# Attention on one core: an order table in place of a planner, a tenth group of exponentials on VectorE, reciprocals as steps of their own, and the last head in two PSUM tiles

## The chip, the cores and the metric

The kernel runs on one core of a Trainium2 chip. The metric is the device time of one execution in microseconds (us), the median of several runs. A profiled execution gives the trace that is read here; its span goes from the first to the last instruction in the trace, and its own time is a little longer than the span.

A core has five engines that run beside each other, each with its own queue in a fixed order. TensorE (PE in the profile; PEld is its weight load) multiplies matrices into PSUM. ScalarE (ACT) computes the exponential. VectorE (DVE) and GpSimd (POOL) do elementwise work; GpSimd works in SBUF here. SyncE (SP) issues the DMA transfers. Engines wait for each other by semaphores.

## The reference

```
batch, heads, seq, dim = 8, 8, 512, 64        # q, k, v in float32
scale = 1.0 / np.sqrt(q.shape[-1])
scores = np.einsum('bhqd,bhkd->bhqk', q, k) * scale
scores = scores - scores.max(axis=-1, keepdims=True)
attn = np.exp(scores)
attn = attn / attn.sum(axis=-1, keepdims=True)
return np.einsum('bhqk,bhkd->bhqd', attn, v).astype(np.float32)
```

There are 64 independent heads. For each, a 512x512 table of scores is made, its exponential taken, and the rows are weighted with v and divided by their sums. The kernel does not subtract the maximum: the division takes out any common factor.

## The kernel before

Heads go in 32 pairs (g = 0 to 31). For a pair, q, k and v are loaded as fp32 (256 KB each, seven buffers each), and POOL casts them to fp16 (`cast`): k and q into one tile `qkp` (five buffers), v into one of twelve tiles `vps`, which have a column of ones beside the 64 columns of v. PE transposes k and q into PSUM (`transposes`, in two parts of four matmuls, part 0 for k, part 1 for q), and VectorE copies both to SBUF as `tqk` (`copy`). Pair 0 has a start of its own (`first_pair`). For pair 1 the two parts have two PSUM tiles and two copies, and the cast of its q is shared: half on VectorE, half on POOL.

Scores are made in *groups* of two 128x512 blocks (`scores`): keys on the partitions, queries along the row, four chunks c of keys per head. There are four groups per pair, 128 in all; the last one is done in two halves of the queries, so that they are numbered 0 to 128. A group's scores lie in one PSUM tile `st`, of which there are three; a fourth group must wait until the first has been read.

For most groups ScalarE takes the exponential from PSUM to a tile `pt` in SBUF (line 516). For a few groups, listed in `ON_DVE`, VectorE does it instead: PE adds a constant by one more matmul (`lift`, line 497), VectorE brings the scores into fixed range (`raise_`, `R`, tile z, line 536) and then makes four *passes* over them (`pass_`, line 553, tiles y and pd), all with fp32 data; a pass reads SBUF and writes SBUF.

The output is made in *units* of 128 queries of a head (`values`): four matmuls add up the chunks, and the column of ones gives the sum of the exponentials. Seven units share a PSUM tile `o`, of which there are two, in banks that the transposes use too. When a tile is full, `normalise` takes the reciprocals of the seven sums and multiplies (lines 566 and 568) into a ring of 56 units in SBUF, and every head that is then complete is stored by a DMA on SP's queue (line 577). The last head (pair 31, second head) has a PSUM tile of its own, taken from the score tiles (`last_values`, line 603): parts 0 and 1 add chunk 0 and 1 for all queries, parts 2 and 3 chunks 2 and 3 for each half of the queries, and `finish` (lines 617 and 618) normalises and stores each half, the first on SP's queue, the second on ScalarE's.

The order in which all of this is issued on each engine is written by a planner in the kernel (`Plan`), which steps through an assumed time, keeps assumed costs and due times, and emits one step after the other. The order on each engine is the order of the emitted steps that use it. `cast_behind` adds to most casts a wait for the VectorE instruction emitted last (`latest`), so that a cast begins at a chosen place between VectorE's instructions. `emit` gives after each cast the load that will use the same buffer, seven pairs later, and `plan.first_loads` is the order of the loads at the start.

Of the kernel before, what the change touches and what calls it, by code (L numbers as in the profile page):

```python
# [17 lines left out]
class Plan:  # L18

    SLOT, EXP, EXP_DONE, EXP_FIXED = 216, 853, 181, 50  # L20
    INTO, OUT_OF = 95, 105
    TRANSPOSE, V_UNIT = 225, 130
    TO_ACT, TO_DVE, TO_PE = 220, 210, 60

    COPY, NORM, RAISE = (601, 690), (307, 390), (1132, 1215)
    COPY_1 = (400, 190)
    NORM_COLUMN, PASS_DONE = 67, 80
    PASS, PASSES = 1133, 4
    OFFSET = 216
    FIRST_EXP = 4915  # L30
    STEP = 5
    CALM, KEEN = 9000, 4
    FIRST_UNIT = 4
    ON_DVE = (8, 24, 35, 41, 61, 68, 80, 94, 111)

    LATE_NORM, LATE_COPY, HURRY, SOON, BACKLOG = 1300, 1400, 900, 80, 1000
    SLACK, AHEAD = 0, 1

    CAST, CAST_DONE, TO_POOL = 557, 130, 150
    FIRST_LAND, LOAD, STORE, LATENCY, ISSUE = 5200, 700, 350, 2300, 450  # L40
    RAW, QK16, NV = 7, 5, 12

    def __init__(self, groups, pairs, first):
        self.groups, self.pairs = groups, pairs
        self.pe, self.act, self.dve = 7000, self.FIRST_EXP, 6300
        self.pool, self.port, self.dma = 4600, 4600, self.FIRST_LAND
        self.m, self.tiled = first, True
        self.read = []
        self.exps = {}
        for m in range(first):  # L50
            self.act += self.EXP + self.EXP_FIXED
            self.exps[m] = self.act + self.EXP_DONE
            self.read.append(self.exps[m])
        self.tq = {0: 5800}
        self.transposed = {0: 5800}
        self.next_t = 1
        self.part_t = 0
        self.banks = [5100, 5800]
        self.todo = [(g, h) for g in range(pairs) for h in range(2)]
        self.last = self.todo.pop()  # L60
        self.last_part = 0
        self.head = None
        self.units = self.FIRST_UNIT
        self.member = {b: m for m, grp in enumerate(groups) for b in grp}
        self.ready = []
        self.passes = []
        self.steps = []
        self.busy_dve = 0
        self.done_heads = 0

        late = {grp[0][0] for m, grp in enumerate(groups) if m in self.ON_DVE}
        due = []
        for g in range(pairs):
            scores = 5000 + 3380 * g
            if g:
                due += [(scores - 2300, g, "k"), (scores - 2290, g, "q")]
            due.append((scores + 4000 + (6000 if g in late else 0), g, "v"))
        self.due = sorted(due)
        self.uncast = list(self.due)
        self.casts = []  # L80
        self.landed, self.cast_done = {}, {}
        self.first_loads = [(g, n) for _, g, n in self.due if g < self.RAW]
        self.first_loads += [(self.RAW, "k"), (self.RAW, "q")]
        for x in self.first_loads:
            self.dma += self.LOAD
            self.landed[x] = self.dma
        self.loads = []
        self.sp = 1650 + 470 * len(self.first_loads)

    def note(self, t, *what):  # L90
        self.steps.append((t, len(self.steps)) + what)

    def emit(self, t, after):
        _, g, n = self.uncast.pop(0)
        shared = (g, n) == (1, "q")
        self.note(t, "cast", g, n, t > self.CALM)
        if not shared:
            self.casts.append((g, n, t if after is None else after + self.TO_POOL))
        if g + self.RAW < self.pairs:
            self.note(t, "load", g + self.RAW, n)  # L100
            self.loads.append(("load", g + self.RAW, n))

    def fits(self, t, soon=0):
        if not self.uncast:
            return False
        _, g, n = self.uncast[0]
        if n != "v" and g >= self.QK16 and self.transposed.get(g - self.QK16, 1e9) > t:
            return False
        return self.landed.get((g, n), 1e9) <= t + soon

    def step_pool(self, t):
        if self.uncast and self.uncast[0][1:] != (1, "q") and not self.casts and self.pool <= t:
            quiet = not self.passes and self.port <= t and not any(x[1] == "raise" for x in self.ready)
            if self.fits(t) and (quiet or self.uncast[0][0] - 1500 < t):
                self.emit(t, None)
        if self.casts and self.pool <= t and self.port <= t:
            g, n, after = self.casts[0]
            if after <= t and self.landed.get((g, n), 1e9) <= t:
                self.casts.pop(0)
                self.pool = t + self.CAST  # L120
                self.port = t + self.CAST
                self.cast_done[(g, n)] = t + self.CAST + self.CAST_DONE

    def step_sp(self, t):
        if not self.loads or self.sp > t:
            return
        what = self.loads[0]
        if what[0] == "load":
            _, g, n = what
            if g >= self.RAW and self.cast_done.get((g - self.RAW, n), 1e9) > t:  # L130
                return
            self.dma = max(self.dma, t + self.LATENCY - self.LOAD) + self.LOAD
            self.landed[(g, n)] = self.dma
        else:
            if what[1] > t:
                return
            self.dma = max(self.dma, t + self.LATENCY - self.STORE) + self.STORE
        self.loads.pop(0)
        self.sp = t + self.ISSUE

    def free(self, n=0):
        m = self.m + n
        if m >= len(self.groups):
            return 1e9
        g = self.groups[m][0][0]
        return max(0 if m < 3 else self.read[m - 3], self.tq.get(g, 1e9))

    def for_dve(self, m):
        return m in self.ON_DVE

    def scores(self, t):
        m, grp = self.m, self.groups[self.m]
        half = m >= len(self.groups) - 2
        slots = 2 if 0 < grp[0][0] and grp[0][2] == grp[1][2] and not half else 1
        on_dve = self.for_dve(m)
        self.note(t, "scores", m, on_dve)
        t += (0 if self.tiled else self.INTO) + self.SLOT * slots
        self.tiled = True
        if on_dve:
            t += self.OFFSET  # L160
            self.ready.append((t + self.TO_DVE, "raise", (m,)))
            self.read.append(1e9)
        else:
            begin = max(self.act, t + self.TO_ACT)
            self.idle = getattr(self, "idle", 0) + begin - self.act
            self.act = begin + self.EXP // (2 if half else 1) + self.EXP_FIXED
            self.exps[m] = self.act + self.EXP_DONE
            self.read.append(self.exps[m])
        self.m += 1
        self.pe = t  # L170

    def full(self, t, cost):
        self.pe = t + cost + (self.OUT_OF if self.tiled else 0)
        self.tiled = False

    def bank(self, t):
        n = min(range(2), key=lambda n: self.banks[n])
        return n if self.banks[n] <= t + 40 else None

    def transposes(self, t):  # L180
        if self.part_t == 0:
            self.bank_t = self.bank(t)
            self.banks[self.bank_t] = 1e9
        self.note(t, "transposes", self.next_t, self.part_t, self.bank_t)
        self.full(t, self.TRANSPOSE)
        self.part_t += 1
        if self.part_t == 2:
            self.transposed[self.next_t] = self.pe + self.TO_DVE
            self.ready.append((self.pe + self.TO_DVE, "copy", (self.next_t, self.bank_t)))
            self.next_t += 1  # L190
            self.part_t = 0

    def wants(self, g, h, part):
        members = [self.member[(g, c, h)] for c in range(4)]
        if (g, h) == self.last:
            end = len(self.groups)
            members = [(members[0], members[1], end - 2, end - 1)[part]]
        exps = max(self.exps.get(m, 1e9) for m in members)
        return max(exps, self.cast_done.get((g, "v"), 1e9))

    def edge(self):

        u, first = self.units, self.FIRST_UNIT
# [15 lines left out]
    def values(self, t):  # L219
        if self.last_values(t):  # L220
            return True
# [563 lines left out]
```

## Time and profile before

| | |
|---|---|
| median of 3 runs | 120.78 us (120.76 to 121.13) |
| profiled execution, its own time | 120.37 us |
| its span | 118.6 us |
| TensorE clock granted, mean | 0.993 |
| DMA | 33.83 MB, mean 285 GB/s |
| exponentials on ScalarE, line 516 | x117, 106.7 us busy |
| passes and raises on VectorE, lines 553 and 536 | x45, 56.4 us busy |
| copies of transposed pairs, line 482 | x30, 20.5 us busy |
| multiplications, line 568, and reciprocals, line 566 | x37 each, 22.6 and 7.3 us busy |
| casts on POOL, lines 435 and 445 | x93, 57.3 us busy |

How to read it: the page gives for each engine its busy time as a share of the span, then groups of instructions by line with their count, total and mean length. A line of the timeline has the start in us, the length in us, the engine, the line of the code, the operation, what it writes and what it reads, and how many instructions are merged; in brackets stands how long the engine was idle just before, and what ended that. An instruction's length is longer than what it costs its engine where the next one starts before it has ended; the distance from start to start is the cost.

### The profile page before, as it was taken

The numbers are of one execution on the slowest core, as the hardware profiler recorded it, in microseconds if no ns is written. First come the engines' busy times: TensorE is split into PE (matmuls) and PEld (weight loads), VectorE is DVE, ScalarE is ACT, GpSimd is POOL, SyncE is SP. The second block draws the span as 40 slices with busy tenths as digits, with TensorE's granted clock in tenths as the row PEclk, the third lists the DMA queues.
The fourth block names the chain that finished last, engine by engine and source line by source line (L and its number), as shares of the span: only waits on it lengthen the run. The fifth ranks groups of instructions, "written<-read, shape, count | busy, mean of one in ns | idle before, by whom it ended". The sixth has DMA issues, their size and how long they took to land.

```text
span 118.6 us, 4088 instructions
## 1 busy us (share of the span) xinstructions
PE 105.0 (89%) x1577; PEld 66.4 (56%) x1577; DVE 103.7 (87%) x179; ACT 111.6 (94%) x124; POOL 57.5 (48%) x102
## 2 busy tenths in 40 slices
PE   7969987999799897989989998998899998998960
PEld 2626554755466454658545574675465674755750
DVE  3453999799999999998999999999999999998560
ACT  4699999999999999999999999999999999999960
POOL 2378731991547722555947255533645436524000
PEclk9999999999999999999999999999999999999997
DMA  3999999999999999999889957999899874231344
GB/s 101 305 352 380 378 380 383 383 379 378 367 302 326 350 365 355 327 371 358 250 297 275 299 169 255 342 364 293 266 309 373 275 253 164 91 122 63 109 163 134
DMA packets 35607, 33.83 MB, mean 285 GB/s; under 512 B 2691, under 2 KB 35587, under 8 KB 35587
## 3 DMA queue, kind: packets, MB, share of 16 engines
q1 hardware_dynamic: 35152, 33.24, 84.8%
q10 hardware_dynamic: 432, 0.33, 0.8%
q8 instruction: 12, 0.20, 0.8%
q14 instruction: 11, 0.07, 0.2%
HBM read 25.17 MB, written 8.39 MB: 283 GB/s over the span
## 4 chain that ended last, share of the span: by engine, by line
ACT 34%; PE 28%; DVE 16%; DMA 11%; issue 6%; SPq 1%; POOL 1%; ACTq 0%
ACT pt L516 32%; PE o L588 10%; PE st L511 10%; DMA k<-in_k_dram 8%; DVE y L553 5%; PE tp L469 4%; DVE tqk L482 3%; DVE ring L568 3%; DMA out_dram<-ring 3%; PE st_0a L636 3%; ACT pt L686 2%; DVE z L536 1%; DVE rc L566 1%; DVE pd L553 1%; SPq L429 1%
## 5 line engine op out<-in xcount | busy, mean ns | idle before, releaser
L516 ACT ACTIVATE pt<-st 128x1024 f16<-128x1024 f32 (+1 forms) x117 | 106.7, 1200 | 0.1
L511 PE MATMUL st<-tqk 64*128 64x512 f16 (+1 forms) x250 | 45.3, 379 | 7.1 <-ACT pt L516 5.4
L588 PE MATMUL o<-vp,pt 128*128 128x65 f16 x936 | 41.7, 194 | 0.0
L588 PEld LDWEIGHTS <-pt 128*128 128x128 f16 x936 | 35.4, 98 | 11.2 <-issue 8.5
L445 POOL CAST qkp<-k 128x512 f16<-128x512 f32 x31 | 19.1, 616 | 20.1 <-DVE y L553 5.5
L435 POOL CAST vp<-v 128x512 f16<-128x512 f32 x32 | 19.7, 619 | 16.6 <-DVE y L553 9.7
L511 PEld LDWEIGHTS <-tqk 64*128 64x128 f16 x250 | 13.7, 93 | 20.9 <-issue 13.8
L445 POOL CAST qkp<-q 128x512 f16<-128x512 f32 x30 | 18.5, 616 | 12.0 <-DVE y L553 7.0
L568 DVE TENSOR_TENSOR ring<-o,rc 128x448 f32<-128x448 f32 (+2 forms) x37 | 22.6, 612 | 1.3
L553 DVE SCALAR_TENSOR_TENSOR y<-y,z 128x1024 f32<-128x1024 f32 x18 | 22.1, 1228 | 0.0
L469 PE MATMUL tp<-ident,qkp 128*128 128x128 f16 x248 | 20.1, 220 | 0.9 <-DVE tqk L482 0.4
L482 DVE COPY tqk<-tp 128x1024 f16<-128x1024 f16 x30 | 20.5, 682 | 0.3 <-PE tp L469 0.3
L469 PEld LDWEIGHTS <-qkp 128*128 128x128 f16 x248 | 14.4, 97 | 8.9 <-issue 4.3
L553 DVE SCALAR_TENSOR_TENSOR y<-z 128x1024 f32<-128x1024 uint16 x9 | 12.1, 1340 | 0.0
L536 DVE TENSOR_SCALAR z<-st 128x1024 f32<-128x1024 f32 x9 | 11.0, 1219 | 1.1 <-PE st L511 0.9
L566 DVE RECIPROCAL rc<-o 128x7 f32<-128x7 f32 (+2 forms) x37 | 7.3, 196 | 4.9 <-PE o L588 4.9
L553 DVE SCALAR_TENSOR_TENSOR pd<-y,z 128x1024 uint32<-128x1024 f32 x9 | 11.2, 1242 | 0.0
L588 PE MATMUL o<-vp,pd 128*128 128x65 f16 x72 | 10.5, 195 | 0.1
L588 PEld LDWEIGHTS <-pd 128*128 128x128 f16 x72 | 7.0, 98 | 1.5 <-issue 0.9
L497 PE MATMUL st<-const-bfloat16-1.0,lift 64*128 64x512 bf16 x18 | 3.5, 383 | 0.5 <-ACT pt L516 0.5
L636 PE MATMUL st_0a<-const-bfloat16-1.0 128*128 128x512 bf16 (+1 forms) x11 | 3.3, 456 | 0.8 <-PEq L769 0.8
L636 PEld LDWEIGHTS <-const-bfloat16-1.0 128*128 128x128 bf16 x15 | 1.6, 122 | 2.4 <-issue 2.4
(48 smaller groups left out, 21.5 us busy)
## 6 DMA issues: line engine op xcount, KB each, us to landing
out_dram<-ring SPq DMA_DIRECT2D x63, 128.0 KB, 4.0
k<-in_k_dram SPq DMA_DIRECT2D x31, 256.0 KB, 5.1
q<-in_q_dram SPq DMA_DIRECT2D x31, 256.0 KB, 5.1
v<-in_v_dram SPq DMA_DIRECT2D x27, 256.0 KB, 5.2
v<-in_v_dram SPq DMA_DIRECT2D x10, 128.0 KB, 3.9
k<-in_k_dram ACTq DMA_DIRECT2D x2, 128.0 KB, 2.9
q<-in_q_dram SPq DMA_DIRECT2D x2, 128.0 KB, 2.7
out_dram<-obl SPq DMA_DIRECT2D x1, 64.0 KB, 1.6
```

What stands on the lines that cost most here:

```text
L435: return nc.gpsimd.tensor_copy(out=vps[g % NV][:, :, :, 0:D], in_=raw[g]["v"][:, :, :, :])
L445: return nc.gpsimd.tensor_copy(out=dst, in_=src[:, :, :, :])
L469: nc.tensor.transpose(tps[g][:, n, i, :], qkp[g][:, n, i, :], ident)
L482: nc.vector.tensor_copy(out=tqk[g][:, :, :], in_=tps.pop(g).rearrange("p n i c -> p n (i c)"))
L511: nc.tensor.matmul(st[:, x, cols], kc, qc[:, cols], start=not on_dve, stop=True)
L516: nc.scalar.activation(out=pt[:, :, cols], in_=st[:, :, cols], func=EXP, scale=scale)
L536: nc.vector.tensor_scalar(out=r["z"][:, :, :], in0=r["st"][:, :, :], scalar1=STEP, scalar2=2.0**17, op0=AluOp.mult, op1=AluOp.max,)
L553: nc.vector.scalar_tensor_tensor(out=r["bits"][:, :, :] if last else r["y"][:, :, :], in0=r["y"][:, :, :] if s else f, scalar=QUARTIC[s], ...
L566: nc.vector.reciprocal(out=rc[:, 0:n], in_=o[:, x : x + n, D : D + 1])
L568: nc.vector.tensor_tensor(out=ring[:, u % NU : u % NU + n, :], in0=o[:, x : x + n, 0:D], in1=rc[:, 0:n].broadcast_to([P, n, D]), op=AluOp. ...
L588: nc.tensor.matmul(os[u // 7][:, u % 7, :], blocks[(g, c, h)][:, y * P : (y + 1) * P], vps[g % NV][:, h, c, :], start=(c == 0), stop=(c == ...
L636: nc.tensor.matmul(dst[:, 0:n], ones[:, 0:P], ones[:, 0:n], start=True, stop=True)
```

## The change

Four things are changed together.

1. `Plan` is taken out. A literal table `ORDER` holds the steps for all engines, and `FIRST` the order of the first loads. A step is a letter and its numbers: `X g.n.behind` cast (n is 0 for k, 1 for q, 2 for v) with its load of pair g + 7, `T` transposes (pair, part, bank), `C` copy, `S m.on_dve` scores, `R` raise, `P m.s` pass, `V` values (pair, head, quarter, unit, bank), `Q` reciprocals and `M` multiplication of a tile's units, `L`, `G` and `F` for the last head. The order on each engine is another one than before in nearly all places.
2. The groups on VectorE are 8, 13, 27, 36, 48, 62, 78, 88, 99 and 108; they were 8, 24, 35, 41, 61, 68, 80, 94 and 111.
3. `normalise` is split into `reciprocals` (`Q`) and `normalise` (`M`), two steps with a place of their own. Either can be the `latest` that a cast waits for.
4. The last head has two PSUM tiles, one for each half of its queries, both taken from the score tiles. Its five parts add chunk 0, chunk 1, and chunks 2 and 3 for the first half, and chunks 0 and 1, and 2 and 3, for the second. Both reciprocals (`G0`, `G1`) come ahead of both multiplications (`F0`, `F1`).

The diff, cut:

```diff
-class Plan:
...
-    ON_DVE = (8, 24, 35, 41, 61, 68, 80, 94, 111)
...
+ORDER = """
+X1.0.0 S3.0 T1.0.1 X1.1.0 T1.1.1 X0.2.0 C1 X3.0.1 X2.0.0 S4.0 V0.0.0.4.1 V0.0.1.5.1 V0.0.2.6.1
+X2.1.0 S5.0 Q4.3 X3.1.1 S6.0 M4.3 T2.0.0 T2.1.0 S7.0 C2 X5.0.1 X4.0.1 X4.1.1 X6.1.1 T3.0.1
+T3.1.1 S8.1 C3 S9.0 R8 X2.2.1 S10.0 S11.0 S12.0 P8.0 X5.1.1 X1.2.1 T4.0.0 T4.1.0 S13.1 C4 X6.0.1
+R13 S14.0 T5.0.0 T5.1.0 V0.0.3.7.1 V0.1.0.8.1 C5 S15.0 S16.0 V0.1.1.9.1 P8.1 X3.2.1 V0.1.2.10.1
...
+V4.0.1.33.0 V4.0.2.34.0 V4.0.3.35.1 S32.0 V5.0.0.36.1 V5.0.1.37.1 Q28.7 X10.0.1 V5.0.2.38.1
+V5.0.3.39.1 M28.7 X11.1.1 X13.1.1 X11.0.1 X12.0.1 X13.0.1 X11.2.1 X8.2.1 V3.1.0.40.1 V3.1.1.41.1
+S33.0 Q35.7 V3.1.2.42.0 M35.7 V3.1.3.43.0 V3.0.0.44.0 V3.0.1.45.0 V3.0.2.46.0 P27.0 X9.2.1
...
+V29.1.3.235.1 S123.0 P108.3 S124.0 S125.0 Q224.7 V27.1.0.236.1 M224.7 V27.1.1.237.1 S126.0
+Q231.7 M231.7 V27.1.2.238.0 V27.1.3.239.0 V30.0.0.240.0 V30.0.1.241.0 V30.0.2.242.0
+V30.0.3.243.0 V30.1.0.244.0 V30.1.1.245.1 V30.1.2.246.1 Q238.7 V30.1.3.247.1 V27.0.0.248.1
+M238.7 V27.0.1.249.1 V27.0.2.250.1 V27.0.3.251.1 S127.0 Q245.7 S128.0 V31.0.0.252.0 M245.7
+V31.0.1.253.0 V31.0.2.254.0 V31.0.3.255.0 L0 L1 L2 Q252.4 L3 M252.4 L4 G0 G1 F0 F1
+"""
+
+FIRST = "1.k 1.q 0.v 2.k 2.q 3.k 3.q 5.k 4.k 4.q 6.q 2.v 5.q 1.v 6.k 3.v 4.v 5.v 6.v 7.k 7.q"
...
-    def cast_behind(g, name, behind):
-        ins = cast(g, name)
-        if behind and latest:
+    def cast_behind(g, n, behind):
+        ins = cast(g, "kqv"[n])
+        if behind:
             tc.add_manual_dep(ins.ins, latest[0].ins.name, SYNC, reason="SBUF ports")
+        if g and g + 7 < NP or n == 2:
+            load(g + 7, "kqv"[n])
...
+    def reciprocals(u, n):
+        rcs[u] = opool.tile([P, 7, 1], FP32, tag="rc", name=f"rc_{u}")
+        x = u % 7
+        dve(nc.vector.reciprocal(out=rcs[u][:, 0:n], in_=os[u // 7][:, x : x + n, D : D + 1]))
+
     def normalise(u, n):
         o, x = os[u // 7], u % 7
-        rc = opool.tile([P, 7, 1], FP32, tag="rc", name=f"rc_{u}")
-        nc.vector.reciprocal(out=rc[:, 0:n], in_=o[:, x : x + n, D : D + 1])
         dve(
             nc.vector.tensor_tensor(
                 out=ring[:, u % NU : u % NU + n, :],
                 in0=o[:, x : x + n, 0:D],
-                in1=rc[:, 0:n].broadcast_to([P, n, D]),
+                in1=rcs.pop(u)[:, 0:n].broadcast_to([P, n, D]),
...
     def last_values(part):
-        if part == 0:
-            o = ps_st.tile([P, 2, S], FP32, tag="st", name="o_last")
-            last["o"] = o[:, 0, 0 : NI * (D + 1)].rearrange("p (x d) -> p x d", x=NI)
-        o = last["o"]
-        for c in (part,) if part < 2 else (2, 3):
-            for x in (range(NI), range(NI), (0, 1), (2, 3))[part]:
+        half = part // 3
+        if part in (0, 3):
+            o = ps_st.tile([P, 2, S], FP32, tag="st", name=f"o_last_{half}")
+            last[half] = o[:, 0, 0 : 2 * (D + 1)].rearrange("p (x d) -> p x d", x=2)
+        for c in ((0,), (1,), (2, 3), (0, 1), (2, 3))[part]:
+            for x in range(2):
+                y = 2 * half + x
...
+    def last_reciprocals(half):
+        rcs[-half] = opool.tile([P, 7, 1], FP32, tag="rc", name=f"rc_last_{half}")
+        dve(nc.vector.reciprocal(out=rcs[-half][:, 0:2], in_=last[half][:, :, D : D + 1]))
+
+    def finish(half):
+        ob = opool.tile([P, 2, D], FP32, tag="obl", name=f"obl_{half}")
...
+        queue = (nc.sync, nc.scalar)[half]
+        queue.dma_start(out=source(out, LAST)[:, 1, 2 * half : 2 * half + 2], in_=ob[:, :, :])
...
-        plan = Plan(groups, NP, 3)
-        steps = plan.run()
         first_loads()
-        for g, name in plan.first_loads:
-            load(g, name)
+        for g, name in (x.split(".") for x in FIRST.split()):
+            load(int(g), name)
...
-        for what, *args in steps:
-            do[what](*args)
+        for step in ORDER.split():
+            do[step[0]](*map(int, step[1:].split(".")))
```

In both orders pair 27 has a group of VectorE's: its chunk 3 (group 111) before, its chunk 0 (group 108) after the change.

## The prediction, made before the changed kernel was run

> **What bounds the kernel now.** I read the page's busy times first, then the order of time engine by engine, the chain that ended last, and the groups by shape for the price of each instruction. Times below are us from the span's start.
>
> ```profile
> PE 105.0 (89%) x1577; PEld 66.4 (56%) x1577; DVE 103.7 (87%) x179; ACT 111.6 (94%) x124; POOL 57.5 (48%) x102
> ```
>
> Two engines are nearly full. The chain says which ends waits last, and it is ScalarE first:
>
> ```profile
> ACT 34%; PE 28%; DVE 16%; DMA 11%; issue 6%; SPq 1%; POOL 1%; ACTq 0%
> ```
>
> ScalarE's row of exponentials has no gap that the view counts:
>
> ```profile
> 7.80 106.75 ACT L516 ACTIVATE pt<-st 128x1024 f16<-128x1024 f32 x117
> ```
>
> It runs 7.80 to 114.55, 90% of the span; what follows is the tail. Looked at one by one, most exponentials start 0.904 after the one before, and where PE is late the interval is longer: 1.42 at 34.08, 1.36 at 110.27, 1.09 at 83.75 and small ones elsewhere, 1.65 in all after group 9. So one exponential less is worth 0.904, and 1.65 of hidden waiting is there to be won or lost again.
>
> VectorE's row, in one stretch, gives its prices:
>
> ```profile
> 69.56 1.22 DVE L553 SCALAR_TENSOR_TENSOR y<-z 128x1024 f32<-128x1024 uint16 x1
> 70.69 0.20 DVE L566 RECIPROCAL rc<-o 128x7 f32<-128x7 f32 x1
> 70.92 0.62 DVE L568 TENSOR_TENSOR ring<-o,rc 128x448 f32<-128x448 f32 x1
> 71.47 1.22 DVE L553 SCALAR_TENSOR_TENSOR y<-y,z 128x1024 f32<-128x1024 f32 x1
> 72.60 1.22 DVE L536 TENSOR_SCALAR z<-st 128x1024 f32<-128x1024 f32 x1
> 73.73 0.68 DVE L482 COPY tqk<-tp 128x1024 f16<-128x1024 f16 x1
> ```
>
> Start to start: a pass 1.13, a raise (z) 1.13, a copy 0.60, a multiplication 0.54, each some 0.08 less than its length, because the next one starts early. Only the reciprocal is different: 0.20 long, 0.228 to the multiplication that waits for its result.
>
> VectorE also loses time to the casts on POOL:
>
> ```profile
> 37.14 0.62 POOL L435 CAST vp<-v 128x512 f16<-128x512 f32 x1
> ...
> 37.19 1.64 DVE L553 SCALAR_TENSOR_TENSOR y<-z 128x1024 f32<-128x1024 uint16 x1
> ```
>
> A pass that begins 0.05 into a cast lasts 1.64 instead of 1.22. z, copies and multiplications (PSUM inputs) beside casts keep their length.
>
> **The change, part by part.** The frame is VectorE's stretch from P8.0 (the first pass) to the last pass, and ScalarE's row.
>
> *Tenth group, ScalarE's side.* One activation less: -0.904. Groups 0 to 7 stay with ScalarE, so exp 9 follows exp 7 as now.
>
> *Start.* Now:
>
> ```profile
> 6.26 0.62 POOL L445 CAST qkp<-k 128x512 f16<-128x512 f32 x1 [1.53 <-DMA k<-in_k_dram]
> 6.90 0.29 DVE L443 CAST qkp<-q 128x256 f16<-128x256 f32 x1 [0.51 <-DMA q<-in_q_dram]
> 6.98 0.81 PE L469 MATMUL tp<-ident,qkp 128*128 128x128 f16 x8
> 7.42 0.84 DVE L476 COPY tqk<-tp 128x512 f16<-128x512 f16 x2 [0.22 <-PE tp L469]
> 8.32 0.94 PE L511 MATMUL st<-tqk 64*128 64x512 f16 x6 [0.52 <-DVE tqk L476]
> 8.99 0.62 POOL L445 CAST qkp<-q 128x512 f16<-128x512 f32 x1
> 9.75 0.62 POOL L435 CAST vp<-v 128x512 f16<-128x512 f32 x1
> ```
>
> The half cast of q1 on VectorE stands ahead of both copies. In the new list it stands between them (T1.0, X1.1, T1.1). The k copy keeps 7.42; the q cast follows at 7.77 and ends 8.06; the second four transposes wait for it (8.10 to 8.50), the second copy runs 8.54 to 8.96, scores 4 from 9.02, exp 4 at 9.45 instead of 8.75: +0.70, straight on ScalarE's row, since exp 3 is done by 8.70. Second, the list casts k3 ahead of k2 and q2. k3 is now the sixth load; the sixth (v1 now) lands by 9.75, and SP's next issues, 0.69 apart, agree with 9.62. POOL works in order, so k2 and q2 wait behind it: k3 9.64, k2 10.20, q2 10.76 to 11.40, where q2 now ends at 9.61. Then second half of T2 11.45 to 11.75, scores 7, T3 12.14 to 12.75, scores 8 and 9 by 13.60 (0.85 for both with the lift, as at 11.20 now), exp 9 at 13.64 instead of 12.38. Sum at the start +1.26. Nothing covers it: three score tiles are all the stock that ScalarE has. If the sixth load came a whole load earlier (0.69), +0.70 would be left; if a load later, +1.95.
>
> *VectorE's stretch.* Raise 8 waits for copy 3 and scores 8: 13.39, ends 14.61; P8.0 then at about 14.7 (14.36 now). From P8.0 to the last pass the new list has 40 passes, 9 raises, 28 copies, 31 multiplications, and 31 reciprocals of which 9 stand right ahead of their own multiplication. The other 22 have independent work behind them. No row shows that: between 0.12 (0.20 less the 0.08 that all other operations overlap) and 0.228 (as now). I take 0.12, since every independent neighbour overlaps. 40x1.13 + 9x1.135 + 28x0.60 + 31x0.54 + 9x0.228 + 22x0.12 = 93.65; at 0.228 it is 96.0. The same sum now is 89.6 (36, 8, 28, and 30 norms of 0.768), measured 94.06 from 14.36 to 108.42: 4.46 lost, of which some 1.9 is waiting for PE, nearly all at 21 to 25 and at 56, where VectorE had no passes in hand, and the rest is passes behind casts. The new list has passes in hand at those places (group 13's between 14 and 25). I take 0.3 for waits and, for casts, 2.1 (as much per pass as now): 2.4 lost. Bounds: 0 and 6. Last pass ends 14.7 + 93.65 + 2.4 = 110.75.
>
> The Trainium skill ("VectorE: DVE Perf Modes", The DRAIN you can't avoid) says the next operation does not start until the pipe is empty; 22 reciprocals apart would then save 0.03 each instead of 0.11 and the last pass would end 1.7 later. The rows above (1.13 between starts of 1.22) disagree, and I go by them.
>
> *What the last pass holds up.* Its tile pd goes into V27.1.0, which stands in PE's order behind scores 125 and ahead of scores 126. ScalarE with no further wait: exp 9 at 13.64, 109 full intervals of 0.904 to 112.18, two halves 0.47 + 0.60: end 113.25. For that exp 126 must start at 111.27, so scores 126 (0.39) at 110.84, after two units of 0.13: last pass by 110.5. It is 0.25 late; ScalarE's own small waits of now (1.65 without the two of half a us) are about 0.6. They overlap, so I take the larger: ScalarE ends 113.85.
>
> *Tail.* Now:
>
> ```profile
> 115.00 0.29 PE L603 MATMUL o_last<-vp,pt 128*128 128x65 f16 x4 [0.46 <-DVE obl L618]
> ...
> 115.61 0.29 DVE L618 TENSOR_TENSOR obl<-o_last,rc_last 128x128 f32<-128x128 f32 x1
> 115.94 0.35 ACTq L625 DMA_DIRECT2D out_dram<-obl  x1
> ```
>
> The last four matmuls wait 0.46 for the reading of the shared tile, and the ring's multiplication stands ahead of the last reciprocal. With two tiles they start 0.07 after the exponential's end and end at +0.36; then reciprocal at +0.42, F0 at +0.54, F1 from +0.75 to +1.04, where it now ends at +1.35: -0.31. (F0 now waits behind the second reciprocal, but its store still lands first.) From there to the span's end 2.70 as now.
>
> *What costs nothing.* Casts, loads and stores keep their number. SP's queue is reordered: 42 loads stand ahead of the first store, 35 now. A store is only needed before its place in the ring, 14 heads later, is written again; loads go out in the time of the first stores, when DMA is full either way (380 GB/s from 10 to 30). What hides a later load is that casts run some pairs ahead; with that cover gone a cast waits, behind it POOL, and the next transposes are late: this is in the range, not in the sum. The list in place of the planner is host work.
>
> **Sum.** Span: 113.85 + 1.04 + 2.70 = 117.6 against 118.6: -1.0. In parts: start +1.26, activation -0.90, tail -0.31, waits 0.6 instead of 1.65. The profiled execution took 120.37, 1.8 around its span; the median of the runs is 120.78. I put the -1.0 against the median: 119.8.
>
> **The rivals.**
>
> *VectorE becomes the bound through the casts (slower).* The place is the passes that find POOL busy. The list queues casts in bunches: seven behind M28, five behind Q182, four behind Q112, and 46 us of casts (83 of 0.56) must fit beside 48.4 us of non-pass work. The point of decision: the last pass 1.6 later than its 110.5, that is 3.8 lost instead of 2.4. With 4.5 lost, as now, the last pass ends 112.85, ScalarE 115.6, span 119.35: 121.5. With 5.2, 122.2. For it: the row of 1.64. Against it: in rows of now the pass starts when the cast is about done, so a bunch should cost one part of a cast and not all of it; but no row has a second cast ready then.
>
> The Trainium skill ("SBUF — State Buffer", Who interferes with whom) calls the shared port pair an exclusive lock, held for the whole instruction by whoever issues first. If POOL's queue won each time, the bunch behind M28 (3.9, less norm 35's 0.77) would cost one pass 3.1. The trace agrees on waiting, up to 0.42; who wins a queue it does not show.
>
> *Nothing to measure.* About 3.8 lost, or the reciprocal at 0.228: the parts cancel, 120.8.
>
> *The start is not paid.* Were exp 9 not late (the loads land early enough, or copies move up), 1.2 more is won: 118.6. Against it: the sixth load's landing, and a cast between two copies.
>
> **Numbers.** Forecast 0.45, start unpaid 0.05, nothing 0.15, VectorE bound 0.35. Within 0.3% (0.36 us) is what a measurement here can't tell from no change. Faster 0.50, same 0.15, slower 0.35. The forecast's own range is 119.2 to 120.4; with the rivals 118.9 to 122.1.
>
> **What would show it.** Right: exp 4 near 9.45 and exp 9 near 13.6; P8.0 near 14.7; a reciprocal of 0.12 before a pass; last pass by 111; 1.0 from ScalarE's end to F1's end. Wrong: passes of 1.4 to 1.7 in dozens, V27 waiting for pd over 1.5, ScalarE's intervals over 1 in the middle; or exp 9 at 12.4.

## The result, and the profile after

The changed kernel takes 131.63 us (median of 4 runs, 130.74 to 132.06) where the kernel before, run beside it, takes 120.81 (120.76 to 121.13): ratio 1.088, 95% interval 1.082 to 1.0939. The forecast was 119.8. The profiled execution took 131.64, its span 129.9, so 11.3 us of span have to be found against the 118.6 of before. In the ratios below, four single executions are left out in which a kernel ran over 1.5% above its own fastest (one of b_front, one of g_less_casts, whose traced run it was, and two of o_old_nine_tiles); the medians count them.

The page's busy times and its rows for ScalarE, VectorE and the granted TensorE clock (40 slices of 3.25 us) show where:

```profile
PE 106.3 (82%) x1579; PEld 67.5 (52%) x1579; DVE 107.8 (83%) x184; ACT 112.3 (86%) x123; POOL 78.9 (61%) x102
...
DVE  3533899999999999999999993037999999999870
ACT  4788799999999999999899990078999999999970
...
PEclk9996899999999999999999996557999999999999
```

The same two rows of the kernel before (slices of 2.97 us):

```profile
DVE  3453999799999999998999999999999999998560
ACT  4699999999999999999999999999999999999960
```

Three things differ. In the 25th and 26th slice, from about 78 to 84 us, ScalarE does nothing and VectorE next to nothing; in the kernel before both are 90% busy or more there. The clock dips in two places. And POOL, with the same 93 casts, is busy 78.9 instead of 57.5.

The chain that ended last no longer begins with ScalarE; DMA and SP's queue are in it:

```profile
DVE 44%; DMA 19%; PE 14%; POOL 7%; issue 6%; SPq 5%; ACT 2%; DVEq 0%; POOLq 0%; ACTq 0%
```

The list of waits (what waits, on what, us in total, times, longest) names the hole:

```profile
POOL vp L186 <- DMA v<-in_v_dram: 10.8, 3, 8.3
ACT pt L269 <- PE st L264: 10.6, 9, 6.5
DVE tqk L235 <- PE tp L222: 10.2, 3, 7.6
...
PE o L344 <- POOL vp L186: 6.9, 1, 6.9
```

Read from the bottom: TensorE waits once, 6.9, for a cast of v; VectorE and ScalarE wait for TensorE; and POOL itself waits 8.3 for a load of v. POOL's timeline there (start, length, what is written and read; the brackets hold the idle time just before and what ended it):

```profile
70.74 0.62 POOL L186 CAST vp<-v 128x512 f16<-128x512 f32 x1 [1.44 <-PE o L344]
71.30 0.62 POOL L196 CAST qkp<-k 128x512 f16<-128x512 f32 x1
71.86 0.62 POOL L196 CAST qkp<-q 128x512 f16<-128x512 f32 x1
80.76 0.62 POOL L186 CAST vp<-v 128x512 f16<-128x512 f32 x1 [8.28 <-DMA v<-in_v_dram]
81.31 0.62 POOL L196 CAST qkp<-q 128x512 f16<-128x512 f32 x1
81.87 0.62 POOL L196 CAST qkp<-k 128x512 f16<-128x512 f32 x1
82.43 1.74 POOL L186 CAST vp<-v 128x512 f16<-128x512 f32 x3
```

By the list these are X20.2, X22.0, X22.1, X22.2, X23.1, X24.0 and X18.2. The cast at 80.76 is that of v22, whose load has only just landed. Nobody reads v22 before unit 192. But POOL works in order, and three places behind it stands v18, which unit 140 reads: the matmul that waited. Why the load is late stands in SP's queue (SPq is its issuing of DMA transfers):

```profile
72.33 1.95 SPq L333 DMA_DIRECT2D out_dram<-ring  x4
74.37 2.45 SPq L178 DMA_DIRECT2D v<-in_v_dram  x2
```

v22 takes the tile of v15, whose cast began at 67.76 and took 1.55, to 69.31. From then to 74.37 SP issues ten other transfers that stand ahead of v22's load in its queue, six of them stores (the last four are the line above). The load, in two halves, is issued from 74.37 on and lands 6 us later. In the list X15.2, which issues this load, and X22.2, which waits for it, stand about three groups of scores apart.

The hole costs more than its length. First the window of 80 to 90 us (busy us of TensorE, its weight loads, VectorE, ScalarE and POOL, then the granted clock, the DMA share and GB/s), then ScalarE's timeline behind the hole:

```profile
80.00:90.00 10.00, 6.90 (x80) 4.38 (x79) 2.63 (x6) 4.24 (x5) 6.04 (x10) 0.55 0.95 313
```

```profile
84.57 1.94 ACT L269 ACTIVATE pt<-st 128x1024 f16<-128x1024 f32 x2 [6.52 <-PE st L264]
87.10 1.94 ACT L269 ACTIVATE pt<-st 128x1024 f16<-128x1024 f32 x2 [0.60 <-PE st L264]
```

After standing still TensorE has a mean clock of 0.55 in this window, and ScalarE waits 0.6 twice more, after every second exponential.

### The profile page after: what moved, and what is told of

The parts are those of the page before. It is cut to its first block, busy times and chain, and to the rows that moved or that the text cites. A ratio compares the mean times of both kernels' runs of the same rounds, so it can differ in the third digit from the quotient of the medians.

```text
span 129.9 us, 4055 instructions
## 1 busy us (share of the span) xinstructions
PE 106.3 (82%) x1579; PEld 67.5 (52%) x1579; DVE 107.8 (83%) x184; ACT 112.3 (86%) x123; POOL 78.9 (61%) x102
## 4 chain that ended last, share of the span: by engine, by line
DVE 44%; DMA 19%; PE 14%; POOL 7%; issue 6%; SPq 5%; ACT 2%; DVEq 0%; POOLq 0%; ACTq 0%
DVE y L306 17%; DMA k<-in_k_dram 11%; DVE tqk L235 8%; DVE z L289 7%; PE o L344 7%; DVE ring L324 6%; DMA v<-in_v_dram 6%; PE st L264 4%; POOL vp L186 4%; DVE pd L306 4%; POOL qkp L196 4%; SPq L180 3%; ACT pt L269 2%; PE tp L222 2%; DVE rc L319 2%
## 5 line engine op out<-in xcount | busy, mean ns | idle before, releaser
L344 PE MATMUL o<-vp,pt 128*128 128x65 f16 x928 | 43.2, 197 | 8.5 <-POOL vp L186 6.9
L344 PEld LDWEIGHTS <-pt 128*128 128x128 f16 x928 | 37.0, 100 | 20.5 <-issue 18.0
L186 POOL CAST vp<-v 128x512 f16<-128x512 f32 x32 | 28.3, 896 | 25.2 <-DMA v<-in_v_dram 10.8
L196 POOL CAST qkp<-q 128x512 f16<-128x512 f32 x30 | 27.3, 923 | 8.8 <-DVE tqk L235 5.4
L196 POOL CAST qkp<-k 128x512 f16<-128x512 f32 x31 | 23.7, 777 | 5.9 <-DMA k<-in_k_dram 3.0
L306 DVE SCALAR_TENSOR_TENSOR y<-y,z 128x1024 f32<-128x1024 f32 x20 | 25.4, 1268 | 0.0
L264 PEld LDWEIGHTS <-tqk 64*128 64x128 f16 x250 | 12.6, 95 | 21.3 <-issue 13.1
L222 PEld LDWEIGHTS <-qkp 128*128 128x128 f16 x248 | 15.4, 101 | 10.5 <-issue 4.3
L306 DVE SCALAR_TENSOR_TENSOR pd<-y,z 128x1024 uint32<-128x1024 f32 x10 | 13.0, 1300 | 0.0
L344 PE MATMUL o<-vp,pd 128*128 128x65 f16 x80 | 12.0, 194 | 0.8 <-DVE tqk L235 0.7
L289 DVE TENSOR_SCALAR z<-st 128x1024 f32<-128x1024 f32 x10 | 12.2, 1216 | 0.1
```

The source lines that it names most:

```text
L186: return nc.gpsimd.tensor_copy(out=vps[g % NV][:, :, :, 0:D], in_=raw[g]["v"][:, :, :, :])
L196: return nc.gpsimd.tensor_copy(out=dst, in_=src[:, :, :, :])
L222: nc.tensor.transpose(tps[g][:, n, i, :], qkp[g][:, n, i, :], ident)
L264: nc.tensor.matmul(st[:, x, cols], kc, qc[:, cols], start=not on_dve, stop=True)
L289: nc.vector.tensor_scalar(out=r["z"][:, :, :], in0=r["st"][:, :, :], scalar1=STEP, scalar2=2.0**17, op0=AluOp.mult, op1=AluOp.max,)
L306: nc.vector.scalar_tensor_tensor(out=r["bits"][:, :, :] if last else r["y"][:, :, :], in0=r["y"][:, :, :] if s else f, scalar=QUARTIC[s], ...
```

## The experiments

Each was timed beside the kernel before on its own chip, so the ratio is what is to be compared.

| label | us, median | ratio to before, 95% interval | span |
|---|---|---|---|
| changed kernel | 131.63 | 1.088 (1.082 to 1.0939) | 129.9 |
| a_v22_after_v18 | 124.99 | 1.0348 (1.0303 to 1.0394) | 122.5 |
| b_front | 131.8 | 1.0892 (1.0828 to 1.0956) | 129.5 |
| c_both | 123.02 | 1.0197 (1.0163 to 1.0231) | 121.1 |
| d_old_order_new_tail | 120.5 | 0.9978 (0.9955 to 1.0002) | 119.0 |
| e_joined | 125.05 | 1.0358 (1.029 to 1.0426) | 123.1 |
| f_nine | 123.09 | 1.0222 (1.0152 to 1.0292) | 120.8 |
| g_less_casts | 122.22 | 1.0117 (1.0059 to 1.0176) | |
| h_two_moves | 121.5 | 1.0078 (1.005 to 1.0106) | 119.7 |
| i_casts_in_gaps | 123.77 | 1.0292 (1.0229 to 1.0356) | 121.7 |
| j_gaps_nine | 124.55 | 1.0352 (1.0306 to 1.0398) | 122.5 |
| k_planner_ten | 123.16 | 1.0231 (1.0199 to 1.0263) | 121.0 |
| l_v13_later | 124.28 | 1.0274 (1.0205 to 1.0343) | 122.7 |
| m_c_nine_tiles | 122.63 | 1.0167 (1.0121 to 1.0213) | 120.7 |
| n_after_nine_tiles | 123.64 | 1.0232 (1.0167 to 1.0297) | 121.6 |
| o_old_nine_tiles | 120.49 | 0.9997 (0.9961 to 1.0033) | 118.2 |

**The hole: two ways to close it.** First the place of one cast.

```diff
-Q119.7 M112.7 X22.1.1 X22.2.1 X23.1.1 X24.0.1 S76.0 M119.7 X18.2.1 S77.0
+Q119.7 M112.7 X22.1.1 X23.1.1 X24.0.1 S76.0 M119.7 X18.2.1 S77.0
...
-X23.2.1 S84.0
+X22.2.1 X23.2.1 S84.0
```

> The changed kernel with one step of its list moved: the cast of v22 (with the load of v29 that goes with it) stands behind the casts of v18 and v19 instead of ahead of them. Theory (a late load blocks POOL's queue): the 8.3 that POOL waits at 72 to 81 for v22's load, with the 6.9 that PE waits there for v18's cast, go, and with them the slow matmuls just after (two intervals of 1.61 between exponentials): about 124, between 122.5 and 125.5. Rival 1 (POOL as a whole is too slow, since its casts are held up by the passes, 79 us busy instead of 57): the wait only moves to another cast, 129 or more. Rival 2 (VectorE's sum is the bound): no earlier than 128, since its last pass does not come earlier.

124.99: 6.6 us less for one cast put behind v18's and v19's. That leaves open whether the place or the late load is to blame. So, with the list of the changed kernel as it is, the loads got nine tiles of each kind instead of seven (FIRST is cut short here):

```diff
-            bufs=7,
+            bufs=9,
...
-        if g and g + 7 < NP or n == 2:
-            load(g + 7, "kqv"[n])
+        if g and g + 9 < NP or n == 2:
+            load(g + 9, "kqv"[n])
...
-FIRST = "1.k 1.q 0.v ... 6.v 7.k 7.q"
+FIRST = "1.k 1.q 0.v ... 6.v 7.k 7.q 7.v 8.k 8.q 8.v 9.k 9.q"
```

> The changed kernel itself, 131.6 us, its list untouched; loads get nine tiles of each kind instead of seven, so every load is issued two pairs of casts earlier, that of v22 after the cast of v13 (at about 52 us) instead of after that of v15 (67.8). Theory (the stall is the late load of v22 in front of v18's cast in POOL's queue): the stall goes though no cast is moved, 124.0 to 125.8 us. Rival (the place of the cast costs whatever the load does): 130 us or more.

123.64, 8.0 less, with no cast moved. POOL's timeline of this kernel, the casts of v22 and v18:

```profile
72.05 1.61 POOL L184 CAST vp<-v 128x512 f16<-128x512 f32 x1
...
74.72 0.61 POOL L184 CAST vp<-v 128x512 f16<-128x512 f32 x1
```

v22 is cast at 72.05 without a wait, and v18 at 74.72 instead of 82.43. Both conditions were needed for the hole: a late load, and an urgent cast queued behind it.

**The start.** The order of the first casts as before:

```diff
-X1.0.0 S3.0 T1.0.1 X1.1.0 T1.1.1 X0.2.0 C1 X3.0.1 X2.0.0 S4.0 V0.0.0.4.1 V0.0.1.5.1 V0.0.2.6.1
-X2.1.0 S5.0 Q4.3
+X1.0.0 S3.0 X1.1.0 T1.0.1 T1.1.1 X0.2.0 C1 X2.0.0 X2.1.0 X3.0.1 S4.0 V0.0.0.4.1 V0.0.1.5.1
+V0.0.2.6.1 S5.0 Q4.3
```

> The changed kernel with the start of the list put right and nothing else: the shared cast of q1 ahead of the first transposes, and the casts of k2 and q2 ahead of k3's. Theory: exp 9 comes some 2.4 earlier (7.0 from exp 3 to exp 9 becomes about 4.6, as in the kernel before), and the late load of v22 moves with it: 129.3. Rival (the load of v22 decides by itself, or VectorE does): the start is swallowed by the wait at 77, 131.2 to 131.9.

Alone it is worth nothing, 131.8, though exp 9 (the exponential of group 9) starts at 12.89 instead of 14.51 (4.5 us behind exp 3 instead of 7.0). The trace shows two places where that goes. The first is a smaller hole of the same kind, which the expectation did not have. POOL waits 3.50 for v13's load and 1.98 for k21's, with the cast of q18 queued behind both, and the transposes of pair 18 wait for that cast:

```profile
59.88 0.40 PE L221 MATMUL tp<-ident,qkp 128*128 128x128 f16 x4 [1.98 <-POOL qkp L195]
```

TensorE's clock is 0.50 from 61.0 to 64.4, and by there b_front is no longer ahead of the changed kernel. The second is v22's load, for which POOL still waits 6.84. Together with a:

> Both edits. Theory: they add up, about 122, and ScalarE or VectorE's last pass decides the rest; 121 to 123.5. Rival 1 and 2 as for the single edits: 127 or more.

123.02, 2.0 less than a. What the start wins comes out only once the hole is gone. With nine tiles it is worth less: from n to m (below), which differ by the start and v22's place, it is 1.0.

**The list and the tail alone.** The order that the planner of before makes, written out as a list, nine groups, every reciprocal ahead of its multiplication; only the last head's two tiles and their steps are new.

> The order of the kernel before (nine groups, each reciprocal right ahead of its multiplication, the old loads), written as a list, and only the last head in two PSUM tiles with the new order of its steps. Theory (the list is host work, the tail gives -0.31): 120.5. Rival (the two tiles or the new order of the last steps cost something, since the first half waits for the second reciprocal): 120.8 to 121.2.

0.9978, and 1 is within the interval: the literal list and the new tail together are worth 0.3, and by the interval between nothing and 0.5. In the traces it takes 3.80 from ScalarE's end to the span's end, 4.05 before. Nothing run here is faster than this by more than the measurement tells.

**VectorE.** Reciprocals back to their multiplications in c_both:

```diff
-V1.1.2.18.0 Q7.7 X4.2.1 X7.0.1 S21.0 M7.7
+V1.1.2.18.0 X4.2.1 X7.0.1 S21.0 Q7.7 M7.7
...
```

> Base: the kernel c_both (new list with the front repaired and the cast of v22 put behind v18's), 123.0 us. Here every reciprocal stands right ahead of its multiplication again. Theory (VectorE is the bound in c_both: its stretch from the first pass of group 8 or 13 to the last pass lost 5.0 us against the sum of its passes, and ScalarE waits for it): 22 reciprocals cost 0.228 instead of 0.12 ahead of a pass, 2.4 us more on VectorE, so 124.5 to 125.5. Rival (the 2.4 us are hidden in waits that VectorE has anyway, ScalarE and the order decide): 122.7 to 123.4.

125.05, 2.0 more, where VectorE's sum grew by 2.4. So time added to VectorE in c_both counts for much, and setting reciprocals apart is the part of the change that gained. How much of the 2.0 is the reciprocals is open: their move also changed what the casts run beside, and the passes took 52.8 us in all instead of 51.3. Then one group less for it:

```diff
-S62.1 M84.7 X14.2.1 C17 S63.0 R62
+S62.0 M84.7 X14.2.1 C17 S63.0
...
-P62.0
...
```

> Base: c_both, 123.0 us. Here group 62 goes back to ScalarE: nine groups on VectorE, the raise and four passes of group 62 (about 5 us of VectorE's work) are left out, ScalarE gets one activation of 0.90 us more. Theory (VectorE, slowed by the casts, is the bound): the 5.0 us that VectorE lost have room now, 119.8 to 121.5. Rival (ScalarE is the bound, with waits that come from the list elsewhere): 123.7 to 124.2.

Neither: 123.09, no change. What ScalarE's intervals have over 0.904 comes to 2.9 in all instead of 5.0, which pays back its extra activation twice over, but the end comes 0.9 later behind its last exponential, with the last stores on SP. VectorE is not the bound here: between its first and last pass it waits 5.5 us for TensorE, in c_both 0.8 us. A list laid out for ten groups does not become one for nine by taking one out. The other way round, the planner of before with the ten groups:

```diff
-    ON_DVE = (8, 24, 35, 41, 61, 68, 80, 94, 111)
+    ON_DVE = (8, 13, 27, 36, 48, 62, 78, 88, 99, 108)
```

> Base: the kernel before itself, 120.5 to 120.7 us, with its planner given the ten groups of the new list (8, 13, 27, 36, 48, 62, 78, 88, 99, 108): ten groups alone. Theory (ten groups cost about 5 us more of VectorE's time than nine, and VectorE had about 3.2 us lost and some 5 us of idle time there, so one activation of 0.90 us goes and new waits of about as much come): 119.9 to 121.0. Rival (VectorE becomes the bound by ten groups in any order): 122 to 123.

The rival: 123.16, 2.5 more, with none of the other changes. (The set is another one, and the planner made another order from it, so the number of groups is not the only thing that differs.) VectorE is full: it waits 0.2 us between its first and last pass. Its timeline at the end:

```profile
113.77 1.22 DVE L553 SCALAR_TENSOR_TENSOR pd<-y,z 128x1024 uint32<-128x1024 f32 x1
```

The last pass starts at 113.77; in the kernel before it was 107.29. Two exponentials of ScalarE wait in the middle (intervals of 2.46 and 1.83), and after the last one VectorE still has work of its own.

**Casts and passes.** From pair 12 on the cast of v converts one of 64 columns; the other columns keep the values of an earlier pair, so this part of the computation is left out.

```diff
+            d = D if g < NV else 1
             return nc.gpsimd.tensor_copy(
-                out=vps[g % NV][:, :, :, 0:D], in_=raw[g]["v"][:, :, :, :]
+                out=vps[g % NV][:, :, :, 0:d], in_=raw[g]["v"][:, :, :, 0:d]
             )
```

> Base: c_both, 123.0 us. From pair NV on the cast of v converts only one of the 64 columns, so most of POOL's v casts, 20 or more of about 0.9 us, are nearly gone; the rest of v is left as it was, so this part of the computation is left out. Theory (a cast and a VectorE pass that meet hold each other up, and VectorE pays part of it: 5.0 us lost against 3.2 before): VectorE's stretch shrinks by 1 to 2 us and the time to 121 to 122.3; means of the passes fall by 20 to 50 ns. Rival (the passes win, POOL alone pays, and POOL is not late): 122.7 to 123.3, means of the passes unchanged.

By the ratios (1.0117 against 1.0197) about 1 us less than c_both, at the edge of what the intervals tell. The theory's other sign, shorter passes, was not measured, so which engine gained is open.

Next the place. A cast waits for the VectorE step ahead of it in the list and runs beside what follows.

```diff
-T3.1.1 S8.1 C3 S9.0 R8 X2.2.1 S10.0 S11.0 S12.0 P8.0 X5.1.1 X1.2.1 T4.0.0 T4.1.0 S13.1 C4
+T3.1.1 S8.1 C3 S9.0 R8 X2.2.1 S10.0 S11.0 S12.0 P8.0 X5.1.1 T4.0.0 T4.1.0 S13.1 X1.2.1 C4
...
```

> Base: c_both, 123.0 us. Every cast waits for the VectorE step ahead of it in the list, so what follows it there runs beside it. In the order of before no cast of the 93 stands ahead of a pass (all stand ahead of a copy, a reciprocal with its multiplication, or a raise); in the new list 28 stand right ahead of a pass or of a reciprocal and a pass. Here the casts of the second part of the list on are moved by up to some 25 steps, in the same order, so that 2 stand so. Theory (that place makes the casts meet passes): POOL's casts come from 0.81 to 0.94 us down towards 0.62 us, VectorE loses 1 to 2 us less than the 5.0 us of c_both, 121 to 122.2 us. Rival (the meetings come from ten groups or from reciprocals apart, or VectorE loses nothing by them): 122.6 to 123.5 us, whatever the casts take.

The theory fell: 123.77, slower, by about as much as the intervals tell. (The casts kept their order but for two, X15.0 and X29.0, which went one place ahead.) POOL's busy time fell from 80.5 to 69.8 as expected, but the passes grew: by the groups of instructions the middle passes have a mean of 1314 ns where c_both has 1234.

```profile
L305 DVE SCALAR_TENSOR_TENSOR y<-y,z 128x1024 f32<-128x1024 f32 x20 | 26.3, 1314 | 0.0
```

The place decides who pays. In the changed kernel a cast that comes 0.20 into a pass is held, 1.49 instead of 0.62 (POOL, then VectorE):

```profile
32.12 1.49 POOL L196 CAST qkp<-q 128x512 f16<-128x512 f32 x1 [0.82 <-POOL qkp L196]
```

```profile
31.92 1.21 DVE L306 SCALAR_TENSOR_TENSOR pd<-y,z 128x1024 uint32<-128x1024 f32 x1
```

In i_casts_in_gaps a pass that comes 0.17 into a cast is held instead, 1.51:

```profile
42.34 0.61 POOL L195 CAST qkp<-q 128x512 f16<-128x512 f32 x1
```

```profile
42.51 1.51 DVE L305 SCALAR_TENSOR_TENSOR pd<-y,z 128x1024 uint32<-128x1024 f32 x1
```

A cast that POOL is made to do late is cheap, as long as nobody waits for it; a pass made late is VectorE's time. With group 62 taken off in this list too:

> Base: i_casts_in_gaps, and group 62 on ScalarE as in f_nine. There nine groups changed nothing (123.09 against 123.02): ScalarE's waits fell by 2.1 us, one activation of 0.90 came back and the end came 1.1 us later for the stores queued on SP. Theory: with casts out of the passes' way VectorE is not the bound with ten groups, so nine make it slower than i_casts_in_gaps by 0.3 to 0.9. Rival (VectorE is still the bound with ten): faster than it by 0.3 or more.

124.55, 0.8 more than i, as the first theory had it, but the two intervals overlap, and its ground, passes left alone by casts, had fallen. Nine groups are no gain in the new order.

**Other late loads.** In c_both POOL waits 2.96 for v13's load with six casts behind it.

```diff
-X13.2.1 S51.0 T15.0.1 P36.1
+S51.0 T15.0.1 P36.1
...
-X21.1.1 X18.1.1 X19.0.1
+X21.1.1 X18.1.1 X13.2.1 X19.0.1
```

> Base: c_both, 123.0 us. There POOL waited 2.96 us at 49.1 to 52.1 for the load of v13, whose cast stands ahead of six casts of k and q; the last of these, the cast of q18, ended late, the transposes of pair 18 waited 0.93 us for it, and ScalarE's intervals after its activations 63 to 65 were 1.90, 1.00 and 1.26 us where 0.904 is one. Here v13's cast stands right behind q18's; its first reader comes some fifty TensorE steps later. Theory (the same blocking of POOL's queue as by v22, only smaller): the three intervals lose 1.0 to 1.4 us, and the time is 121.5 to 122.1. Rival (VectorE is the bound, and the wait comes back some groups later): 122.6 to 123.3.

A miss: 124.28. POOL's timeline shows the wait handed on to the next load in its queue, that of k21:

```profile
56.41 0.98 POOL L195 CAST qkp<-k 128x512 f16<-128x512 f32 x1 [3.71 <-DMA k<-in_k_dram]
```

Another 1.1 us of ScalarE's were lost at 19 us, behind another late load; up to there the list is c_both's own, whose trace has no such loss, so not all of the difference is the edit's. So the loads were made earlier altogether, c_both with nine tiles for them:

> c_both, 123.0 us, with nine tiles of each kind for loads. In c_both POOL's casts waited 9.8 us for loads in the middle of the kernel, each time with other casts queued behind. Theory (these waits make transposes and so ScalarE late): POOL's waits for loads fall under 3 us, ScalarE's intervals lose 1 to 2.5 us, 120.8 to 122.0. Rival (VectorE with ten groups is the bound): POOL's waits go too, and the time stays at 122.5 to 123.3.

122.63: mostly the rival's answer. The waits of POOL's casts for loads fall only from 9.8 to 6.2 over the whole kernel, those for v from 5.9 to 0.7, and the time by some 0.4, less than the intervals tell apart. The waits did not fall under 3 us, so the run does not price what late loads cost c_both. And the same for d:

> d_old_order_new_tail, 120.5 us beside 120.67 of before, with nine tiles of each kind for loads. No cast there waits long for a load with others behind it, so both theories expect little: 120.2 to 120.7. If the loads taken ahead hold up the first ones, it is slower by up to 0.5.

No change, 0.9997.

**A try at a faster one.** In d, three steps of scores moved ahead of waits of half a microsecond:

```diff
-V7.1.2.58.0 X11.0.1 X11.1.1 Q49.7 M49.7 V7.1.3.59.0 V6.0.0.60.0 V6.0.1.61.0 V6.0.2.62.0 S35.1
-X8.2.1 Q56.7 M56.7 S36.0 T10.0.1
+S35.1 V7.1.2.58.0 X11.0.1 X11.1.1 Q49.7 M49.7 V7.1.3.59.0 V6.0.0.60.0 S36.0 V6.0.1.61.0
+V6.0.2.62.0 X8.2.1 Q56.7 M56.7 T10.0.1
...
-V27.1.0.240.1 V27.1.1.241.1 V27.1.2.242.1 V27.1.3.243.1 S125.0 S126.0
+S125.0 V27.1.0.240.1 V27.1.1.241.1 V27.1.2.242.1 V27.1.3.243.1 S126.0
```

> Base: d_old_order_new_tail (order of before as a list, nine groups, last head in two tiles), 120.5 us beside 120.67 of before. Here three steps of score matmuls are moved ahead: those of group 35 by four matmul steps, those of group 36 by about four, those of group 125 by four. In d ScalarE's interval after its 35th activation was 1.45 us and after its 125th 1.36 us where 0.904 is one activation. Theory (the order of TensorE's work alone sets these two waits): both go, 0.9 us less, 119.4 to 119.8. Rival (the waits move to the next groups, because a score tile is free no earlier): 120.3 to 120.7.

Slower than the kernel before by 0.78%, not faster. The interval behind group 34's exponential (the 35th activation of the expectation) is still 1.40, and two new ones of 1.41 and 1.25 follow it; the one near the end is gone. The waits moved on, as the rival had it, and one more came.

## Why the prediction was wrong, point by point

**The step that failed** is "What costs nothing". It named the mechanism, a cast that waits for a later load, "behind it POOL, and the next transposes are late", and put it "in the range, not in the sum", on the cover that "casts run some pairs ahead". The cover was not checked cast by cast. For v22 the list leaves three groups between the cast that frees its tile and its own cast, and ten transfers, six of them stores, stand between on SP. Seven tiles of each kind are a budget, and a list that casts v22 ahead of v18 spends it. In the sum the step is worth 6.6 (a) to 8.0 us (n) instead of nothing; the range's upper end had no term of that size.

**The start** was right in mechanism and mis-sized. The interval from exp 3 to exp 4 grew by 0.69, from 0.95 to 1.64 (forecast 0.70), and k3's cast started at 9.57 when its load landed (forecast 9.64). But exp 9 came 7.00 after exp 3, not 4.58 + 1.26: the step took 2.42. The other 1.2 us fall where TensorE's clock is 0.50, from 10.5 to 13.9. Windows of TensorE alone (from and to, length, busy us, instructions, granted clock, DMA share, GB/s):

```profile
7.00:8.00 1.00, 0.28 (x6) 1.00 0.97 338
8.00:9.00 1.00, 0.48 (x6) 1.00 1.04 361
...
11.00:12.00 1.00, 1.00 (x10) 0.50 1.10 386
12.00:13.00 1.00, 1.00 (x8) 0.50 1.09 383
```

TensorE had little to do from 7 to 9, and when the work came its clock was 0.50; the eight transposes of pair 2 took 1.17, where the kernel before takes 0.61. The traces of a and n, with the same start, show the same fall. In c_both it is busy 1.31 of those 2 us, the clock stays at 1.00, and exp 9 starts at 12.88. That the idle time brought the fall is read from these traces, not tested by itself. The start is worth 2.0 us of time (a to c), 1.0 with nine tiles (n to m).

**VectorE's stretch.** The prices held: a reciprocal apart starts its follower after 0.12.

```profile
24.19 0.20 DVE L319 RECIPROCAL rc<-o 128x7 f32<-128x7 f32 x1
24.31 1.18 DVE L306 SCALAR_TENSOR_TENSOR y<-z 128x1024 f32<-128x1024 uint16 x1
```

e_joined agrees with its worth, as far as it goes. The 2.4 lost did not hold. It was too low by its own figures: of the 4.46 lost before, 1.9 was put down to waiting, which leaves 2.56 for 36 passes behind casts, and 40 at that rate are 2.8 and not 2.1; and the trace of before has 1.2 of waits in the stretch, not 1.9. In the changed kernel the stretch from P8.0 (15.55) to the end of the last pass (121.5) is 12 us over the sum of 93.65, 8.4 of it in waits around the hole. In c_both, without the hole, it is 98.6 from 13.88 to 112.50: 5.0 lost, on the rival's side of the point of decision (3.8). Of these, 2.5 are passes longer than 1.22 (51.3 us for 40) and 0.8 waits, 0.5 of it for transposes. So the rival, VectorE as the bound, is what is left in c_both when the hole is closed: VectorE hardly waits there, and what e adds to it counts. k shows that these ten groups fill VectorE in the planner's order too: the activation taken from ScalarE is worth 0.90, and the net is 2.5 the other way. That the number of groups alone does it is not shown, since f, with nine in the new list, is no faster. The rival's own reason, casts in bunches, finds no support where it was looked at: the two passes beside the bunch behind M28 took 1.22 and 1.27, since POOL waited.

The Trainium skill ("SBUF — State Buffer", Who interferes with whom) says that whoever issues first holds the shared port pair for the whole instruction, and that issue order decides who blocks. The two pairs of rows above, 1.49 for a cast and 1.51 for a pass, agree with it.

**ScalarE and the tail.** One activation less: 116 rows instead of 117. From ScalarE's end (125.93) to F1's end it took 0.99 (forecast 1.04), but from there to the span's end 2.94 instead of 2.70, so that only 0.1 of the forecast 0.31 is left in the changed kernel; in d 0.25 is. ScalarE's waits after exp 9 (what its intervals have over 0.904), put at 0.6, are 11.8 in the changed kernel, 6.6 of it in the one interval of the hole, and 4.5 in c_both.

**What stays open.** Of the 10.8 us the hole is 6.6 to 8.0 and the start 1.0 to 2.0; 2.0 (m) to 2.4 (c) remain. In c_both's trace what remains is one activation less (-0.9), 2.8 more of ScalarE's waits after exp 9 than before, exp 9 later by 0.5, and an end as long as before (4.10 against 4.05). How much of these waits is the ten groups and how much the new order is not shown: k points to the groups, f to the order. Why nine groups in the new list (f, j) do no better than ten was read from ScalarE's intervals and the end, but no list laid out anew for nine was tried.

## What to carry to other kernels

On an engine that works in order, a prefetched item whose data may be late must not stand ahead of an urgent one; check for every such item how far its place is from the place that frees its buffer, and what else is in the queue that issues its load. Before giving a nearly full engine more work, take its sum to the deadline with the losses it shows now, not with fewer. Repairs do not add up: the start was worth nothing while later holes set the end, and 1.0 to 2.0 us once the largest was closed.

## What the hardware showed unexpectedly

TensorE's granted clock fell to 0.50 not only after the 6.9 us without matmuls (back to 1.00 about 6 us after work resumed) but also some 2 us after a stretch in which it was busy 0.76 of 2 us; with 1.31 of 2 us busy (c_both) it stayed at 1.00. In b_front it fell at 61.0, after 2 us with next to no matmuls (57.9 to 59.9). Where it turns is not known: j_gaps_nine was busy 0.84 of the 2 us from 7 to 9 and stayed at 1.00. The Trainium skill ("TensorE: Matmul & The Clock Gate", The HAM clock gate) gives half rate after an idle window of about 3.4 us; the first case agrees, and in the others the traces show no window of that length without matmuls.

A cast and a pass that meet do not share: the one that comes second is held to about the other's end, and the sum of busy time moves between POOL and VectorE (80.5 and 108.5 us in c_both, 69.8 and 110.4 in i_casts_in_gaps).
